# Last down chunk of a two-layer decoder trunk: half of its columns as seven products, in a fixed order

## The chip, the core and the metric

The kernel runs on one core of one Trainium2 chip. The metric is the device time in microseconds of one execution; lower is better. The kernel before was timed three times: 2022.12, 2022.2 and 2024.6 us, median 2022.2 us.

A core has engines with queues of their own: TensorE (PE in the rows, PEld for its weight loads) multiplies, VectorE (DVE) and ScalarE (ACT) work elementwise, GpSimd (POOL) and SyncE (SP) here mostly issue DMAs. Each engine works its queue in the order in which the program was built; engines wait for each other by semaphores.

## What is computed

Two layers over 256 rows of width 2048, in float32. Each layer is a norm, a projection, two mixers, an output projection and a feed-forward part:

```
x = x + mix @ w_out[l]
h = rmsnorm(x, norm2_g[l])
u = jnp.square(jax.nn.relu(h @ w_up[l]))     # 256 x 8192
x = x + u @ w_down[l]                        # 8192 x 2048
```

The change concerns the last line, in both layers.

## The kernel before, in words

**Blocks.** Every weight matrix is cut into blocks of 512 x 512 (four 128-row tiles). A block is loaded by SP (`fetch`, four blocks ahead), then split by `prep` into a rounded half `wh` (two casts on ACT) and the rest `wl` (one subtraction on DVE), because the product is made of three terms: high by high, high by low and low by high. Three sets of `wh` and `wl` exist (`WBUFS`), so the split of block i+3 starts when block i's matmuls have ended.

**Up.** `block_a` computes a block of h @ w_up in 16 matmuls of 512 columns and 16 of 256. Four blocks make 512 columns of u; `up_sum` adds their parts (ACT copies `us`, DVE sums into `ur`), `up_square` applies relu and square on ACT.

**Down.** The 8192 rows of w_down are 8 chunks of 1024; a chunk c needs the u of up parts 2c and 2c+1. A plain block (`block_b`) takes 24 matmuls of 512 columns: 12 for the first 128 rows of u (T = 0), 12 for the second (T = 1). In chunks 0 to 6 the work is cut otherwise: for each half p of the 2048 output columns the chunk is a 2 x 2 by 2 x 2 block product that is made of seven products of 12 matmuls each (`product`, `block_p`) in place of eight. For this DVE and ACT make sums. Of u: `S1`, `S2`, `S3`, `S4` and the splits into high and low halves (`11`, `12`, `22`, `s1` to `s4`, tiles `a...` and `as...`). Of the weights, in a `Super` with four quarter tiles `qx`, `qw`, `qy`, `qz`: the sums x+y and t = (x+y)+z on DVE, and y+z and t+w as accumulating DMAs from POOL's queue. After a product DVE adds its result to x (`add_to`).

**Order.** `BETWEEN` is the order of 22 steps that goes round for each chunk (0 is an up block, other numbers are products, 20 and more belongs to the next chunk). `BESIDE` says after which of these steps each sum, split or load is issued. The chunks 0 to 6 run in a stretch whose order on DVE, ACT, PE and POOL is fixed as written (`manual_schedule`). What stands outside of it is ordered by the scheduler of the language when the kernel is built.

**Last chunk, before.** Chunk 7 has no products: its eight blocks (four column groups n, two row halves kb) are plain `block_b` calls, outside of the fixed stretch, with accumulators in turn from two PSUM pools. Steps of chunk 6 that would start chunk 7's products are left out. After each n DVE adds to x, and in the last layer ACT issues the store of x; in layer 0 the next layer's norm begins (`nxt.chunk(n)`: PE transposes x into bank `hb`, ACT and DVE make the two halves of `hi`, ACT squares x into `jki`).

**Start of the feed-forward part.** The first two up parts run alone, then the product (0, 0, 1), then the weight sums x+y and t of `supers[l, 0, 0]` are issued, then the fixed stretch begins. In that stretch the entry ("t", 0, 22) of `BESIDE` makes t of chunk 0 once more, so this sum stands twice in DVE's queue.

Of the kernel before, what the change touches and what calls it, by code (L numbers as in the profile page):

```python
# [8 lines left out]
F32 = mybir.dt.float32  # L9
F32R = mybir.dt.float32r  # L10
# [7 lines left out]
P = 128  # L18
S = 256
NT = S // P  # L20
# [29 lines left out]

BETWEEN = (0, 0, 2, 0, 5, 6, 0, 7, 3, 0, 11, 4, 0, 15, 0, 16, 13, 12, 17, 0, 21, 14)
NU = len(BETWEEN)
BESIDE = (("up", 0, 6), ("sq", 0, 8), ("load x", 0, 11), ("11", 13), ("S3", 13),
# [8 lines left out]
def trunk(ctx, tc, x, norm1_g, w_in, q_norm_g, k_norm_g, attn_sinks, gla_gate_w,  # L62
          gla_gate_b, gla_norm_g, w_out, norm2_g, w_up, w_down, out):
    nc = tc.nc
# [7 lines left out]
    def bank(name):  # L72
        return misc.tile([P, 512], F32, tag="m", name=name)


    blocks, supers, forms = [], {}, {}
# [59 lines left out]
    for c in range(7):  # L136
        ups = [("up", i, kb) for i in (2 * c + 2, 2 * c + 3) for kb in range(4)]
        if c == 0:
            FFN_ORDER.append(("product", 0, 0, 1))
        for step in BETWEEN:  # L140
            if step == 0:
                FFN_ORDER.append(ups.pop(0))
            elif step < 20 or c < 6:
                FFN_ORDER.append(("product", c + step // 20, step // 10 % 2, step % 10))
    FFN_ORDER += [("down", 7, n, kb) for n in range(4) for kb in range(2)]
    for l in range(DEPTH):
        plan(l)
    NB = len(blocks)
# [58 lines left out]
    now = [0]  # L207

    def add(gen, at):
        side.append([at, gen])  # L210
# [14 lines left out]
    def block_b(accs, lhs, first, last, kts):  # L225

        i = next_block()
        n = blocks[i][2][1] - blocks[i][2][0]
        wh, wl = halves.pop(i)
        for T in range(NT):  # L230
            for k in range(4):
                if kts is None:
                    ah, al = lhs[T][:, k, 0], lhs[T][:, k, 1]
                else:
                    a = lhs[kts[k]]
                    ah = a[:, T * P:(T + 1) * P]
                    al = a[:, S + T * P:S + (T + 1) * P]
                o = accs[T][:, :n]
                nc.tensor.matmul(o, ah, wh[:, k, :n], start=(first and k == 0), stop=False)  # L239
                nc.tensor.matmul(o, ah, wl[:, k, :n], start=False, stop=False)  # L240
                nc.tensor.matmul(o, al, wh[:, k, :n], start=False,  # L241
                                 stop=(last and k == 3))
            if T or n > 264:
                tick()
        prep_to(i + 1 + WBUFS)
# [52 lines left out]
    xs = {}  # L298
# [74 lines left out]
    class Norm:  # L373


        def __init__(self, name, gcols, g0, var):
            self.name, self.gcols, self.g0, self.var = name, gcols, g0, var
            self.ss = sm.tile([P, NT, 4], F32, tag="ss", name=f"ss{name}")
            self.hT = {}
            self.r = None  # L380

        def part(self, n, pr):
            b = bank(f"hb{self.name}{n}{pr}")
# [21 lines left out]
        def chunk(self, n):  # L405
            for pr in range(2):
                self.gain(n, pr, self.part(n, pr))
                yield 1
            self.squares(n)
            if n == 3:  # L410
                yield 1
                self.r = self.rvar() if self.var else self.rstd()

# [453 lines left out]
    def feed_forward(l, norm2):  # L867
# [13 lines left out]
        def up_square(i):  # L881
            nc.scalar.activation(ur[i], ur[i], AF.Relu)
            nc.scalar.activation(ur[i], ur[i], AF.Square)

        def split(name, c, src, tag=None):
            d = fp.tile([P, 4, 2, P], F32R, tag=f"a{tag or name}", name=f"a{name}{l}{c}")
            nc.scalar.activation(d[:, :, 0], src, AF.Copy)
            nc.vector.tensor_tensor(d[:, :, 1], src, d[:, :, 0].bitcast(F32), ALU.subtract)  # L888
            a[name, c] = d

        def beside(c, what, which=0):

            if what == "up":
                up_sum(2 * c + which)
                return
            if what[:4] == "load":
                if c < 7:
                    supers[l, c, which].load(what[5])
                return
            if what == "sq":  # L900
                up_square(2 * c + which)
                return
            if "x" in what or "t" in what or "y" in what:
                if c < 7:
                    supers[l, c, which].sum(what)
                return
            u1, u2 = ur[2 * c], ur.get(2 * c + 1)
            a11, a21 = (u1[:, :, T * P:(T + 1) * P] for T in range(NT))
            if u2 is not None:
                a12, a22 = (u2[:, :, T * P:(T + 1) * P] for T in range(NT))  # L910
            if c == 7:
                if what == "S3":
                    split("21", c, a21, "s1")
                elif what in ("11", "12", "22"):
                    split(what, c, {"11": u1, "12": u2, "22": u2}[what]
                          [:, :, (what == "22") * P:][:, :, :P])
            elif what == "11":
                split(what, c, a11)
            elif what == "S3":
                nc.vector.tensor_tensor(a21, a11, a21, ALU.subtract)  # L920
            elif what == "s3":
                split(what, c, a21)
            elif what == "12":
                split(what, c, a12)
            elif what == "22":
                split(what, c, a22)
            elif what == "S2":
                t = fp.tile([P, 4, P], F32, tag="s2", name=f"s2{l}{c}")
                nc.vector.scalar_tensor_tensor(t, a22, -1.0, a21, ALU.mult, ALU.subtract)
                a["S2", c] = t  # L930
            elif what == "S1":
                nc.vector.tensor_tensor(a11, a["S2", c], a11, ALU.add)
            elif what == "S4":
                nc.vector.tensor_tensor(a12, a["S2", c], a12, ALU.add)
            else:
                split(what, c, {"s1": a11, "s2": a["S2", c], "s4": a12}[what])
# [39 lines left out]
        def go(k0, steps, c0):  # L976

            for k, step in enumerate(steps):
                if step[0] == "up":
                    up(*step[1:])  # L980
                else:
                    product(*step[1:])
                for b in BESIDE:
                    if b[-1] == k0 + k:
                        beside(c0 + 1, *b[:-1])
                    elif b[-1] - NU == k0 + k:
                        beside(c0, *b[:-1])

        ffn = list(FFN_ORDER)
        for i in range(2):  # L990
            for kb in range(4):
                up(*ffn.pop(0)[1:])
                if i == 0 and kb == 1:
                    supers[l, 0, 0].load("xwyz")
            up_sum(i)
            if i == 0:
                nc.vector.tensor_scalar(nr, norm2.r, -1.0, None, ALU.mult)
            up_square(i)
        for b in BESIDE:
            if 8 < b[-1] < NU and b[0] not in ("up", "sq", "x+y", "t") and b[0][:4] != "load":  # L1000
                beside(0, *b[:-1])
        product(*ffn.pop(0)[1:])
        supers[l, 0, 0].sum("x+y")
        supers[l, 0, 0].sum("t")
        with tc.manual_schedule(engines={mybir.EngineType.DVE, mybir.EngineType.Activation,
                                         mybir.EngineType.PE, mybir.EngineType.Pool}):
            for c in range(7):
                n = NU if c < 6 else NU - 1
                go(0, ffn[:n], c)
                del ffn[:n]  # L1010
        beside(7, "22")
        for step in ffn:
            _, c, n, kb = step
            if kb == 0:
                accs = [bank(f"dn{l}{c}{n}{T}") if n % 2 == 0 else
                        acc.tile([P, 512], F32, tag="a", name=f"dn{l}{c}{n}{T}")
                        for T in range(NT)]
            block_b(accs, [a[f"{T + 1}{kb + 1}", c] for T in range(NT)], kb == 0, kb == 1,
                    None)
            if kb == 0:  # L1020
                continue
            for T in range(NT):
                add_to(n, T, accs[T])
                if nxt is None:
                    nc.scalar.dma_start(
                        out[0, T * P:(T + 1) * P, n * 512:(n + 1) * 512], xs[T, n])
            if nxt is not None:
                add(nxt.chunk(n), now[0] + 2)
        return nxt

    norm = Norm("i0", n1cols, 0, False)
# [10 lines left out]

    def start():
        norm.squares(0)
        yield 3
        other_cols()

# [30 lines left out]
```

## Time and profile before

| what | value |
|---|---|
| median of 3 runs | 2022.2 us |
| the profiled execution's own time | 2022.15 us |
| its span, first to last instruction | 2020.4 us |
| PE busy | 2006.2 us, 99% of the span, 10238 matmuls |
| PEld busy | 1694.7 us, 84% |
| DVE busy | 1603.7 us, 79% |
| ACT busy | 1219.2 us, 60% |
| mean granted TensorE clock | 1.000 |
| HBM traffic | 189 GB/s over the span |

The share of busy time is a mean over stages. In the 40 slices of the span DVE's busy tenths are 5 to 7 in the mixers and 8 to 9 in the feed-forward parts. Matmuls overlap: a matmul of 512 columns is shown with 0.39 us, but the next one starts 0.23 us after it, so the step from start to start is what a matmul costs. The same holds, less strongly, on DVE and ACT, whose next instruction starts some 0.09 us before the last one's shown end.

### The profile page before, as it was taken

How to read it: one execution, taken by the hardware profiler on the slowest of the kernel's cores; microseconds unless marked ns; L12 is line 12 of the kernel's file. 1: busy time of each engine (PE TensorE's matmuls, PEld its weight loads, DVE VectorE, ACT ScalarE, POOL GpSimd, SP SyncE). 2: the span in 40 equal slices, each digit the busy share in tenths (PEclk: the TensorE clock that was granted, in tenths of full speed). 3: DMA queues.
4: the chain of work that ended last, by engine and by line, in shares of the span. 5: the costliest groups of instructions: out<-in, count | busy, mean ns of one | idle time of the engine just before them, and what ended most of it. 6: DMA issues, size and time to landing. Idle time of an engine off the chain costs nothing.

```text
span 2020.4 us, 25911 instructions
## 1 busy us (share of the span) xinstructions
PE 2006.2 (99%) x10238; PEld 1694.7 (84%) x10238; DVE 1603.7 (79%) x1452; ACT 1219.2 (60%) x1685; POOL 100.2 (5%) x142
## 2 busy tenths in 40 slices
PE   9999999999999999999999999999999999999999
PEld 7877888888888888888888878888888888888887
DVE  5676565789899998999656765657899999999994
ACT  5575454666666666666555655546666666666663
POOL 3200000000000000000012000000000000000000
PEclk9999999999999999999999999999999999999999
DMA  7554367677878878887555443666877889878874
GB/s 237 173 179 146 108 208 247 202 241 228 288 234 256 262 243 264 240 256 223 188 189 165 160 157 127 201 237 208 255 244 251 248 251 288 244 243 256 236 212 166
DMA packets 205384, 442.59 MB, mean 219 GB/s; under 512 B 7460, under 2 KB 15728, under 8 KB 198096
## 3 DMA queue, kind: packets, MB, share of 16 engines
q1 hardware_dynamic: 194976, 378.82, 53.9%
q0 software_dynamic: 8512, 58.96, 15.7%
q10 hardware_dynamic: 1776, 3.16, 0.4%
q8 instruction: 80, 1.31, 0.3%
q14 instruction: 40, 0.33, 0.0%
HBM read 380.10 MB, written 2.10 MB: 189 GB/s over the span
## 4 chain that ended last, share of the span: by engine, by line
PE 93%; DMA 2%; DVE 2%; ACT 2%; issue 1%; SPq 0%; DVEq 0%; ACTq 0%
PE up L255 22%; PE up L261 11%; PE dn L278 9%; PE dn L276 9%; PE dn L274 9%; PE in L240 6%; PE in L239 6%; PE in L241 6%; PE wo L240 3%; PE wo L241 3%; PE wo L239 3%; PE dn L240 1%; PE dn L241 1%; DMA raw<-in_w_up_dram 1%; PE dn L239 1%; ACT wh L180 1%
## 5 line engine op out<-in xcount | busy, mean ns | idle before, releaser
L185 DVE TENSOR_TENSOR wl<-raw,wh 128x2048 fp32r<-128x2048 f32 (+1 forms) x252 | 560.4, 2224 | 266.6 <-ACT wh L180 262.6
L180 ACT ACTIVATE wh<-raw 128x1024 fp32r<-128x1024 f32 (+2 forms) x516 | 500.8, 1018 | 290.4 <-PE in L241 73.6
L255 PE MATMUL up<-hf,wh 128*128 128x512 f32 x2048 | 504.5, 390 | 0.0
L255 PEld LDWEIGHTS up<-hf,wh 128*128 128x128 f32 x2048 | 376.1, 188 | 71.8
L261 PEld LDWEIGHTS up<-hf,wl 128*128 128x128 f32 x2048 | 275.6, 190 | 18.5 <-DVE wl L185 0.2
L261 PE MATMUL up<-hf,wl 128*128 128x256 f32 x2048 | 281.4, 282 | 0.0
L240 PE MATMUL in<-wl,hi 128*128 128x512 f32 (+1 forms) x640 | 237.2, 372 | 0.4 <-DVE wl L185 0.4
L239 PE MATMUL in<-wh,hi 128*128 128x512 f32 (+1 forms) x640 | 237.6, 374 | 0.0
L241 PE MATMUL in<-wh,hi 128*128 128x512 f32 (+1 forms) x640 | 234.4, 370 | 0.0
L276 PE MATMUL dn<-wl,as 128*128 128x512 f32 x448 | 175.0, 391 | 0.0
L274 PE MATMUL dn<-wh,as 128*128 128x512 f32 x448 | 174.9, 390 | 0.0
L278 PE MATMUL dn<-wh,as 128*128 128x512 f32 x448 | 174.6, 390 | 0.0
L180 ACT ACTIVATE wh<-qx 128x1024 fp32r<-128x1024 f32 x112 | 112.4, 1053 | 49.3 <-DVE qx L97 23.1
L240 PEld LDWEIGHTS in<-wl,hi 128*128 128x128 f32 x640 | 120.1, 188 | 22.4 <-issue 1.5
L239 PEld LDWEIGHTS in<-wh,hi 128*128 128x128 f32 x640 | 120.0, 188 | 21.4 <-issue 1.0
L185 DVE TENSOR_TENSOR wl<-qx,wh 128x2048 fp32r<-128x2048 f32 x56 | 128.1, 2287 | 11.4 <-ACT wh L180 11.4
L241 PEld LDWEIGHTS in<-wh,hi 128*128 128x128 f32 x640 | 119.9, 188 | 20.1 <-issue 0.8
L180 ACT ACTIVATE wh<-qt 128x1024 fp32r<-128x1024 f32 x112 | 112.1, 1050 | 37.4 <-PE up L255 23.3
L278 PE MATMUL dn<-wh,a 128*128 128x512 f32 x336 | 131.2, 391 | 3.4 <-DVE a L888 3.4
L276 PE MATMUL dn<-wl,a 128*128 128x512 f32 x336 | 131.3, 391 | 0.0
L274 PE MATMUL dn<-wh,a 128*128 128x512 f32 x336 | 131.2, 390 | 0.0
L185 DVE TENSOR_TENSOR wl<-qt,wh 128x2048 fp32r<-128x2048 f32 x56 | 128.1, 2287 | 1.3 <-ACT wh L180 1.3
(203 smaller groups left out, 2813.5 us busy)
## 6 DMA issues: line engine op xcount, KB each, us to landing
raw<-in_w_up_dram SPq DMA_DIRECT2D x128, 1024.0 KB, 7.3
raw<-in_w_in_dram SPq DMA_DIRECT2D x62, 1024.0 KB, 5.1
raw<-in_w_out_dram SPq DMA_DIRECT2D x32, 1024.0 KB, 5.0
qx<-in_w_down_dram SPq DMA_DIRECT2D x28, 1024.0 KB, 6.6
qw<-in_w_down_dram SPq DMA_DIRECT2D x28, 1024.0 KB, 5.3
qy<-in_w_down_dram SPq DMA_DIRECT2D x28, 1024.0 KB, 7.6
qz<-in_w_down_dram SPq DMA_DIRECT2D x28, 1024.0 KB, 10.1
qy<-qz POOLq DMA_DIRECT2D x28, 1024.0 KB, 8.2
```

The costliest lines, as they stand in the source:

```text
L180: nc.scalar.activation(wh[:, ks, :n], src[:, ks], AF.Copy)
L185: nc.vector.tensor_tensor(wl[:, :, :n], src, wh[:, :, :n].bitcast(F32), ALU.subtract)
L239: nc.tensor.matmul(o, ah, wh[:, k, :n], start=(first and k == 0), stop=False)
L240: nc.tensor.matmul(o, ah, wl[:, k, :n], start=False, stop=False)
L241: nc.tensor.matmul(o, al, wh[:, k, :n], start=False, stop=(last and k == 3))
L255: nc.tensor.matmul(accs[f], wh[:, k, f * P:(f + 1) * P], rhs[kts[k]], start=(first and k == 0), stop=False)
L261: nc.tensor.matmul(accs[f][:, :S], wl[:, k, f * P:(f + 1) * P], rhs[kts[k]][:, :S], start=False, stop=(last and k == 3))
L274: nc.tensor.matmul(o, ah, wh[:, k], start=(first and k == 0), stop=False, skip_group_check=not first)
L276: nc.tensor.matmul(o, ah, wl[:, k], start=False, stop=False, skip_group_check=not first)
L278: nc.tensor.matmul(o, al, wh[:, k], start=False, stop=(last and k == 3), skip_group_check=not first)
```

## The change

**Chunk 7, columns 1024 to 2047 (p = 1).** They are now made of seven products, as in the chunks before. Product 1 of it stands in chunk 6's round (the step 21 of `BETWEEN`, which was left out before). The columns 0 to 1023 (n = 0 and 1) stay plain blocks. The order of the rest is written out in `LAST`: plain (n 0, kb 0), product 2, plain (0, 1), products 5 and 6, plain (1, 0), products 7 and 3, plain (1, 1), product 4. `BESIDE_LAST` says which sums and splits are issued after each of these ten steps. All of it is inside the fixed stretch. The loads, sums and splits of `BESIDE` now hold for chunk 7 too. All plain accumulators come from one pool. The row split `21` of chunk 7 gets a tile of the `ur` ring.

**Next norm.** It takes the column groups as they are done: 0, 3, then 1 and 2, and counts chunks in place of looking for n = 3.

**Start.** The splits and the difference `11`, `S3`, `s3` of chunk 0 are written right behind the first `up_square`, and the first of the two sums t is gone.

The core of the diff:

```
+LAST = ((0, 0), 2, (0, 1), 5, 6, (1, 0), 7, 3, (1, 1), 4)
+BESIDE_LAST = (("t", "S1", "y+z", "22"), ("s1", "s2"), ("S4",), ("s4",), ("t+w",))
...
-            elif step < 20 or c < 6:
-                FFN_ORDER.append(("product", c + step // 20, step // 10 % 2, step % 10))
-    FFN_ORDER += [("down", 7, n, kb) for n in range(4) for kb in range(2)]
+            else:
+                c1 = c + step // 20
+                FFN_ORDER.append(("product", c1, 1 if c1 == 7 else step // 10 % 2, step % 10))
+    FFN_ORDER += [("product", 7, 1, u) if type(u) == int else ("down", 7, *u) for u in LAST]
...
             up_square(i)
+            if i == 0:
+                for what in ("11", "S3", "s3"):
+                    beside(0, what)
...
         supers[l, 0, 0].sum("x+y")
-        supers[l, 0, 0].sum("t")
...
+            accs = {}
+            for k, step in enumerate(ffn):
+                done = {7: [(3, 1)], 3: [(3, 0)], 4: [(2, 0), (2, 1)]}.get(step[-1], [])
+                if step[0] == "product":
+                    product(*step[1:])
+                else:
...
+                    block_b(accs[n], [a[f"{T + 1}{kb + 1}", c] for T in range(NT)], kb == 0,
+                            kb == 1, None)
...
+                for b in BESIDE_LAST[k:k + 1]:
+                    for what in b:
+                        beside(7, what)
```

DVE's queue in layer 1 at the end of chunk 6 and the begin of chunk 7, before (names: `x` the residual rows, `wl` and `wh` the halves of a block, `a12` and `a22` splits of u):

```order
L941 SCALAR_TENSOR_TENSOR x1_2_109<-dn1611_15574,vf1_10991,x1_2_109 128x512
L185 TENSOR_TENSOR wl446_15861<-raw446_15793,wh446_15860 128x2048
L185 TENSOR_TENSOR wl447_15903<-raw447_15845,wh447_15902 128x2048
L888 TENSOR_TENSOR a1217_15867<-ur115_15832,a1217_15867 128x4x128
L888 TENSOR_TENSOR a2217_15871<-ur115_15832,a2217_15871 128x4x128
L185 TENSOR_TENSOR wl448_15934<-raw448_15876,wh448_15933 128x2048
```

The same place now (`qx`, `qt` the weight sums, `s2` the sum S2):

```order
L190 TENSOR_TENSOR wl449_15893<-qw171_15801,wh449_15892 128x2048
L101 TENSOR_TENSOR qx171_15636<-qx171_15636,qy171_15761 128x2048
L895 TENSOR_TENSOR a1217_15900<-ur115_15863,a1217_15900 128x4x128
L942 SCALAR_TENSOR_TENSOR x1_2_109<-dn1611_15597,vf1_11016,x1_2_109 128x512
L190 TENSOR_TENSOR wl450_15917<-raw450_15877,wh450_15916 128x2048
L930 SCALAR_TENSOR_TENSOR s217_15921<-ur115_15863,ur114_15498 128x512
L190 TENSOR_TENSOR wl451_15950<-qx171_15636,wh451_15949 128x2048
L104 TENSOR_TENSOR qt171_15954<-qx171_15636,qz171_15739 128x2048
L933 TENSOR_TENSOR ur114_15498<-s217_15921,ur114_15498 128x4x128
L895 TENSOR_TENSOR a2217_15958<-ur115_15863,a2217_15958 128x4x128
L942 SCALAR_TENSOR_TENSOR x0_2_107<-dn1712_15961,vf1_11016,x0_2_107 128x512
L190 TENSOR_TENSOR wl452_15978<-qt171_15954,wh452_15977 128x2048
```

The split `a22` stood right behind `a12`; now an add, two block subtractions, S2, the weight sum t and S1 stand between them, and the weight sum x+y stands ahead of both.

ACT's queue in layer 0 where the next norm begins, before (`hi` the next norm's columns, `jki` its squares):

```order
L402 ACTIVATE jki100_8045,ssi1_2877<-x0_0_89 128x512
L180 ACTIVATE wh223_8003<-raw223_7931 128x1024 x2
L402 ACTIVATE jki101_8047,ssi1_2877<-x1_0_91 128x512
L402 ACTIVATE jki110_8137,ssi1_2877<-x0_1_98 128x512
L180 ACTIVATE wh224_8049<-raw224_7966 128x1024 x2
L369 ACTIVATE hi10_7997<-hbi100_7992,n1cols_118 128x256
L402 ACTIVATE jki111_8139,ssi1_2877<-x1_1_100 128x512
L369 ACTIVATE hi11_8000<-hbi100_7992,n1cols_118 128x256
L369 ACTIVATE hi12_8027<-hbi101_8022,n1cols_118 128x256
L180 ACTIVATE wh225_8095<-raw225_8008 128x1024 x2
```

And now:

```order
L374 ACTIVATE hi10_8061<-hbi100_8056,n1cols_118 128x256
L374 ACTIVATE hi11_8064<-hbi100_8056,n1cols_118 128x256
L185 ACTIVATE wh226_8067<-qz071_7738 128x1024 x2
L374 ACTIVATE hi12_8092<-hbi101_8087,n1cols_118 128x256
L374 ACTIVATE hi13_8095<-hbi101_8087,n1cols_118 128x256
L407 ACTIVATE jki100_8110,ssi1_2877<-x0_0_89 128x512
L407 ACTIVATE jki101_8112,ssi1_2877<-x1_0_91 128x512
L185 ACTIVATE wh227_8114<-raw227_8041 128x1024 x2
```

In both orders up to four small steps stand between two casts `wh`. Before, all blocks here were plain, with 24 matmuls each; now `wh225`, `wh226` and `wh227` belong to products 7 and 3, with 12 matmuls each, and to the plain block (1, 1).

## Rows read from the trace of the kernel before

**Rows 1.** The cores: span, and mean granted TensorE clock.

```profile
core 0: 2020.4 us, clock 1.000
```

**Rows 2.** The page's first part: busy us (share of the span) xinstructions.

```profile
PE 2006.2 (99%) x10238; PEld 1694.7 (84%) x10238; DVE 1603.7 (79%) x1452; ACT 1219.2 (60%) x1685; POOL 100.2 (5%) x142
```

**Rows 3.** PE's waits: engine line, waited for: us in total, times, longest.

```profile
PE dn L278 <- DVE a L888: 3.4, 2, 1.9
...
PE dn L240 <- DVE wl L185: 1.3, 2, 0.7
```

**Rows 4.** Timeline of PE, layer 1's end: start, us, line, out<-in [idle <-releaser].

```profile
1958.13 0.39 PE L274 MATMUL dn<-wh,a 128*128 128x512 f32 x1
...
1960.85 0.39 PE L274 MATMUL dn<-wh,as 128*128 128x512 f32 x1
...
1969.16 0.63 PE L239 MATMUL dn<-wh,a 128*128 128x512 f32 x2
...
1977.37 0.61 PE L239 MATMUL dn<-wh,a 128*128 128x512 f32 x2
1978.64 0.50 PE L240 MATMUL dn<-wl,a 128*128 128x512 f32 x1 [0.66 <-DVE wl L185]
1978.97 0.40 PE L241 MATMUL dn<-wh,a 128*128 128x512 f32 x1
```

**Rows 5.** Timeline of DVE, the same stretch.

```profile
1962.72 0.74 DVE L941 SCALAR_TENSOR_TENSOR x<-dn,vf,x 128x512 f32<-128x512 f32 x1
1963.38 2.28 DVE L185 TENSOR_TENSOR wl<-qt,wh 128x2048 fp32r<-128x2048 f32 x1
...
1970.93 2.29 DVE L185 TENSOR_TENSOR wl<-raw,wh 128x2048 fp32r<-128x2048 f32 x1 [2.40 <-ACT wh L180]
1973.14 1.69 DVE L878 TENSOR_TENSOR ur<-up,us 128x256 f32<-128x256 f32 x4
1974.74 0.74 DVE L941 SCALAR_TENSOR_TENSOR x<-dn,vf,x 128x512 f32<-128x512 f32 x1
1976.29 2.29 DVE L185 TENSOR_TENSOR wl<-raw,wh 128x2048 fp32r<-128x2048 f32 x1 [0.81 <-ACT wh L180]
```

**Rows 6.** Timeline of DVE, layer 0, begin of the feed-forward part's fixed stretch.

```profile
387.27 2.28 DVE L100 TENSOR_TENSOR qt<-qx,qz 128x2048 f32<-128x2048 f32 x1
...
395.53 0.68 DVE L929 SCALAR_TENSOR_TENSOR s<-ur,ur 128x512 f32<-128x512 f32 x1
398.41 2.29 DVE L185 TENSOR_TENSOR wl<-raw,wh 128x2048 fp32r<-128x2048 f32 x1 [2.20 <-ACT wh L180]
400.62 2.29 DVE L100 TENSOR_TENSOR qt<-qx,qz 128x2048 f32<-128x2048 f32 x1
402.82 0.69 DVE L932 TENSOR_TENSOR ur<-s,ur 128x512 f32<-128x512 f32 x1
403.42 0.69 DVE L888 TENSOR_TENSOR a<-ur,a 128x512 fp32r<-128x512 f32 x1
```

**Rows 7.** Timeline of ACT, the same stretch.

```profile
396.37 2.01 ACT L180 ACTIVATE wh<-raw 128x1024 fp32r<-128x1024 f32 x2 [1.43 <-DMA raw<-in_w_up_dram]
```

**Rows 8.** Timeline of PE, the same stretch.

```profile
401.84 0.40 PE L276 MATMUL dn<-wl,a 128*128 128x512 f32 x1
...
404.17 0.50 PE L278 MATMUL dn<-wh,a 128*128 128x512 f32 x1 [1.93 <-DVE a L888]
```

**Rows 9.** Timeline of ACT, layer 0's end, next norm's steps.

```profile
986.30 0.63 ACT L402 ACTIVATE jki<-x 128x512 f32<-128x512 f32 x1 [3.02 <-DVE x L941]
...
997.17 0.84 ACT L369 ACTIVATE hi<-hbi,n1cols 128x256 fp32r<-128x256 f32 x2 [1.78 <-DVE hi L370]
```

**Rows 10.** Timeline of DVE, the same stretch.

```profile
997.68 0.88 DVE L370 SCALAR_TENSOR_TENSOR hi<-hbi,n1cols,hi 128x256 fp32r<-128x256 f32 x2 [0.54 <-ACT hi L369]
```

**Rows 11.** Waits between 960 and 1030 us: total, times, longest.

```profile
ACT hi L369 <- DVE hi L370: 6.6, 3, 2.4
```

**Rows 12.** Timeline of PE, the same stretch: six of the next norm's transposes.

```profile
992.90 0.81 PE L387 MATMUL hbi<-ident,x 128*128 128x128 f32 x6
```

**Rows 13.** The page's DMA issues: engine, count, KB each, median us to landing.

```profile
qy<-qz POOLq DMA_DIRECT2D x28, 1024.0 KB, 8.2
```

More of the change, by code (lines that the diff above doesn't have):

```diff
@@ L379, in __init__ @@
             self.hT = {}
-            self.r = None
+            self.r, self.chunks = None, 0
         def part(self, n, pr):
@@ L409, in chunk @@
             self.squares(n)
-            if n == 3:
+            self.chunks += 1
+            if self.chunks == 4:
                 yield 1
@@ L885, in split @@
         def split(name, c, src, tag=None):
-            d = fp.tile([P, 4, 2, P], F32R, tag=f"a{tag or name}", name=f"a{name}{l}{c}")
+            d = fp.tile([P, 4, 2, P], F32R, tag=tag or f"a{name}", name=f"a{name}{l}{c}",
+                        bufs=3 if tag else 1)
             nc.scalar.activation(d[:, :, 0], src, AF.Copy)
@@ L896, in beside @@
             if what[:4] == "load":
-                if c < 7:
-                    supers[l, c, which].load(what[5])
+                supers[l, c, 1 if c == 7 else which].load(what[5])
                 return
@@ L903, in beside @@
             if "x" in what or "t" in what or "y" in what:
-                if c < 7:
-                    supers[l, c, which].sum(what)
+                supers[l, c, 1 if c == 7 else which].sum(what)
                 return
@@ L910, in beside @@
                 a12, a22 = (u2[:, :, T * P:(T + 1) * P] for T in range(NT))
[L911 to L917, printed above, removed]
+            if c == 7 and what == "S3":
+                split("21", c, a21, "ur")
+            if what == "11":
                 split(what, c, a11)
@@ L998, in feed_forward @@
             up_square(i)
+            if i == 0:
+                for what in ("11", "S3", "s3"):
+                    beside(0, what)
         for b in BESIDE:
-            if 8 < b[-1] < NU and b[0] not in ("up", "sq", "x+y", "t") and b[0][:4] != "load":
+            if 8 < b[-1] < NU and b[0] in ("12", "S2"):
                 beside(0, *b[:-1])
@@ L1007, in feed_forward @@
             for c in range(7):
[L1008 to L1028, printed above, removed]
+                go(0, ffn[:NU], c)
+                del ffn[:NU]
+            accs = {}
[4 more added lines that the diff above has]
+                else:
+                    _, c, n, kb = step
+                    if kb == 0:
+                        accs[n] = [acc.tile([P, 512], F32, tag="a", name=f"dn{l}{c}{n}{T}")
+                                   for T in range(NT)]
+                    block_b(accs[n], [a[f"{T + 1}{kb + 1}", c] for T in range(NT)], kb == 0,
+                            kb == 1, None)
+                    done = [(n, T) for T in range(NT)] if kb else []
+                    for n, T in done:
+                        add_to(n, T, accs[n][T])
+                for b in BESIDE_LAST[k:k + 1]:
+                    for what in b:
+                        beside(7, what)
+                for n, T in done:
+                    if nxt is None:
+                        nc.scalar.dma_start(
+                            out[0, T * P:(T + 1) * P, n * 512:(n + 1) * 512], xs[T, n])
+                if nxt is not None and done and step[-1] != 7:
+                    add(nxt.chunk(done[0][0]), now[0] + 2)
         return nxt
@@ L1044, in start @@
         norm.squares(0)
+        norm.chunks += 1
         yield 3
```

## Prediction, made before the changed kernel was timed

> **What bounds the kernel now.** I read the cores' line first, for the clock and the span [rows 1], then the shares [rows 2]: TensorE is busy for 99% of the span, VectorE for 79%. The profiled execution took 2022.15 us around a span of 2020.4 us, and 2022.15 is within 0.1 us of the median of the three runs, so sums made against it hold for the median. Next I read PE's waits [rows 3]. In the two feed-forward parts there are two kinds: twice 1.9 us until a split of u is ready, at the begin of the fixed stretch, and twice 0.7 us until a `wl` is ready, in chunk 7. Everything else is matmul after matmul, so a matmul removed is worth its step, as long as nobody is late. Then I read the stretch that is changed, in layer 1, engine by engine. On PE a product of 12 matmuls takes 2.72 us from start to start (1958.13 to 1960.85), 0.227 each; a plain block of 24 takes 5.44 [rows 4]. On DVE a subtraction `wl` or a weight sum takes 2.20 us of its queue (400.62 to 402.82), an add to x 0.66 (1962.72 to 1963.38), a sum or split of u 0.60 (402.82 to 403.42) [rows 5, 6]. So a product costs PE 2.72 us, and DVE one `wl` and one add, 2.86 us, before any sum is made. DVE has slack only because plain blocks and up blocks stand between the products.
>
> **What is removed.** Per layer 192 matmuls become 84 + 96 = 180: 12 x 0.227 = 2.72 us saved, 5.44 us for both. The old wait of PE in chunk 7 goes too: from 1977.37 two matmuls are due within 0.45, and the third starts at 1978.64, so 0.82 us, with 0.10 more because the step after a wait is 0.33 in place of 0.23 [rows 4]: 0.92 per layer.
>
> **What is added to DVE's queue, layer 1.** I follow DVE's and PE's queues forward from 1969.16, where the last up block ends and nothing has changed yet. PE now does product (7,1,1) to 1971.88, product 4 of chunk 6 to 1974.60, plain (0,0) to 1980.04. On DVE the rows from 1970.93 to 1976.29 stay, as the same steps stand there in the same order, a `wl` last [rows 5]. Then, back to back: x+y at 1978.49, `a12` at 1980.69, ready with 0.69 and 0.06 until PE sees it (as 403.42 to 404.17 [rows 6, 8]) at 1981.44. Product 2 wants it for its third matmul at 1980.50: PE waits **0.94**, and the product ends at 1983.81. DVE goes on: add 1981.29, `wl` of plain (0,1) 1981.95, S2 1984.15, `wl` of product 5 1984.75, weight sum t 1986.95, S1 1989.15, `a22` 1989.75, visible at 1990.50. Plain (0,1) wants its `wl` at 1984.04 and gets it at 1984.30 (**0.26**); it wants `a22` for its second half at 1987.35 and gets it at 1990.50 (**3.15**). It ends at 1992.87. Product 5 wants the low half of `as1` at 1993.33. DVE's `wl` ahead of it cannot start before ACT has cast the sum t, 1989.28 to 1991.29 (a cast takes 2.01 [rows 7]), so `as1` comes at 1994.28 (**0.95**). Behind that I find no wait: product 6 and the plain blocks give DVE time. The waits come to 5.30, with four late steps of 0.10 to 5.7 us. Layer 1: 5.7 - 0.92 - 2.72 = **+2.1 us**.
>
> **Layer 0** has the same, +2.1, and then the next norm in the same queues. Two more places:
> - Plain (1,1). After `as1` DVE makes `as2` and, behind its cast, a `wl` at 1995.0. From the adds at 1997.2 (on layer 1's clock) I count: two adds, S4, an add, a `wl`, a split, an add, 6.04 us; a half of `hi`, 0.52; ACT's next half, 0.36; a cast, 2.03; a `wl`, 2.20; `hi` on DVE, 0.52, and on ACT, 0.36; two squares, 1.26 [rows 9]; a cast, 2.03; a `wl`, 2.33. This is 2014.9. ACT and DVE take turns on a bank of `hi`, as they do now: ACT waited three times for DVE's half, 6.6 us in all, once 1.78, and DVE for ACT's 0.54 [rows 9 to 11]. PE wants that `wl` at 2011.4: product 5 ends at 1996.65, then come product 6, plain (1,0), products 7 and 3 (2.72 + 5.44 + 2.72 + 2.72 = 13.60), eight transposes, 0.9 [rows 12], and one matmul. PE waits **3.5 us**.
> - The next layer's first block. Columns n = 1 and 2 are now the last to be done, and the block needs n = 1 second. From the restart at 2014.85 PE has 5.3 + 2.72 + 5.44 us of matmuls, 2.6 of transposes, and wants the second n = 1 tile 1.8 later, at 2032.7. DVE must do five `wl`, five adds, five halves of `hi` and 0.7 of small steps first: 17.0 us, to 2031.8, which alone would cost nothing. With the turns of ACT and DVE (each of three casts stands behind a `hi` or a square, and the `wl` behind it) I come to 2036.9: **4.2 us**. The ends of this term are 0 and 4.2; I take 4.2, since such turns cost waits in rows of before.
>
> Layer 0: 2.1 + 3.5 + 4.2 = **+9.8 us**.
>
> **Edits that cost nothing.** The removed sum t (387.27) frees 2.2 us of DVE, but DVE then stands idle 2.20 us at 398.41 for a cast which waits for a DMA of an up block [rows 6, 7]. The sum that stays, at 400.62, is the one right ahead of the late split, so PE's wait there, 2.1 us (401.84 + 0.23 to 404.17 [rows 8]), stays. Its ends are 0 and 4.2 us gained for both layers; I take 0. The earlier `11`, `S3`, `s3` change no order in any queue. The two more accumulating DMAs per layer land some 8.2 us after their issue [rows 13]; in the queue their readers come 15 us later and more. SP loads as many blocks as before, four quarters in place of four blocks. The store at the very end is one add and one DMA behind the last matmul, as before.
>
> **Sum.** 2022.15 + 2.1 + 9.8 = **2034 us**. Its own range is 2030 to 2038: the 4.2 of the norm partly saved, or each of seven waits longer by half a microsecond.
>
> **Rivals.**
> A. *TensorE stays the bound.* Then the saved matmuls and the old waits are all: 2022.15 - 5.44 - 1.84 = 2014.9, or 2010.7 if the waits at the start go as well. For it speaks the share of 99% against 79% [rows 2]; against it that the 79% is a mean, and that the order puts seven DVE steps between `a12` and `a22`. It decides at plain (0,1): DVE would have to be 3.15 us earlier there, more than one `wl`. The Trainium skill (Perfetto Trace Analysis, Identifying the Most-Contended Engine) says to take the engine of highest occupancy first; by that rule the time would fall, as here. No row speaks for its use over a stretch where the product's 2.72 us meet 2.86 us of DVE.
> B. *The next norm hides as it does now.* Only the waits in front of it stay, in both layers: 2022.15 + 4.2 = 2026.4. For it: before, PE lost nothing to the norm's steps. Against it: they stood beside blocks of 5.44 us, now beside products.
> C. *The clock falls.* The granted clock was 1.000 throughout [rows 1], the higher level of 2.4 GHz, and stayed there over PE's waits of 1.9 us. Three new waits are over 3 us. If the lower level held for one plain block after each, 24 x 0.227 = 5.4 us each, it would be 2039 with one and 2050 with three. The Trainium skill (TensorE: Matmul & The Clock Gate, Why this matters for your kernels) warns of idle gaps between bursts of matmuls that take the clock to half; no row here shows a fall.
>
> **How the numbers follow.** Forecast 0.72, A 0.08, B 0.10, C 0.07, and 0.03 that gains and waits cancel. Within 0.2% (4 us) is about what a measurement of this kernel can tell from no change. Faster: A, 0.08. Same: 0.03 and a third of B, 0.06. Slower: the rest, 0.86. The range, 2028 to 2041, holds the forecast, a part of B and the milder part of C, and leaves A and the worst of C out.
>
> **What would show it.** In the new profile PE's matmuls are 24 fewer. PE's waits should name DVE: `a` or `as` splits four times with the longest over 3 us in each layer, and a `wl` and `hi` in layer 0 alone. DVE should have no idle time from the sum x+y to `a22` (12 us). Layer 0's part should account for some 10 us of the loss and layer 1's for 2. I am wrong if PE has no wait over 1 us in chunk 7, if the time is under 2026, or if the clock is below 1.000 in the windows behind the waits.

## The result and the profile after

| | before | after |
|---|---|---|
| median | 2022.7 us | 2041.5 us (2038.4 to 2043.0) |
| ratio | | 1.009, 95% interval 1.0078 to 1.0102 |
| profiled execution, its own time | 2022.15 us | 2038.39 us |
| mean granted TensorE clock, profiled execution | 1.000 | 0.998 |

(The median of before is that of the executions beside the changed kernel.) The change costs 18.8 us. The forecast was 2034 with a range of 2028 to 2041: the sign is right, the profiled execution lies inside, the median half a microsecond above the top. (The kernel before, too, took half a microsecond more beside this measurement than the 2022.15 us that the forecast was added to: 2022.15 + 18.8 = 2041.0, the top itself.)

The page of the changed kernel, its cores' line and its shares; they answer to [rows 1, 2]:

```profile
core 0: 2036.3 us, clock 0.998
...
PE 2005.0 (98%) x10214; PEld 1689.8 (83%) x10214; DVE 1635.3 (80%) x1482; ACT 1234.6 (61%) x1705; POOL 106.2 (5%) x146
```

TensorE has the 24 matmuls less, and the kernel is longer all the same. The shares have hardly moved, so the loss isn't to be read there. It is in PE's waits, which answer to [rows 3] (columns: who waits, for whom, us in total, times, longest):

```profile
PE dn L283 <- DVE a L895: 6.2, 4, 2.6
PE dn L246 <- DVE a L895: 5.9, 2, 3.0
...
PE dn L245 <- DVE wl L190: 2.8, 1, 2.8
PE in L246 <- DVE hi L375: 2.3, 2, 1.2
PE in L244 <- ACT hi L374: 1.0, 1, 1.0
PE dn L283 <- DVE as L895: 0.8, 1, 0.8
PE dn L279 <- DVE x L944: 0.4, 1, 0.4
PE dn L244 <- ACT wh L185: 0.3, 1, 0.3
```

The old `wl` wait [rows 3] is gone, and the new ones are those that the prediction had listed, plus two small ones, for x and for a cast `wh`. The wait for the split `as1`, however, is there once only, in layer 0. DVE's queue in layer 1 answers to [rows 5]: from x+y to `a22`, nine instructions without a gap (no brackets), 1990.01 to 2001.96.

```profile
1990.01 2.29 DVE L101 TENSOR_TENSOR qx<-qx,qy 128x2048 f32<-128x2048 f32 x1
1992.21 0.69 DVE L895 TENSOR_TENSOR a<-ur,a 128x512 fp32r<-128x512 f32 x1
...
1998.48 2.28 DVE L104 TENSOR_TENSOR qt<-qx,qz 128x2048 f32<-128x2048 f32 x1
2000.68 0.68 DVE L933 TENSOR_TENSOR ur<-s,ur 128x512 f32<-128x512 f32 x1
2001.28 0.68 DVE L895 TENSOR_TENSOR a<-ur,a 128x512 fp32r<-128x512 f32 x1
```

And PE's queue there, which answers to [rows 4] (start, duration, instruction; in brackets the wait and who ended it). These are plain block (0,1)'s second half and, for comparison, the same place in layer 0:

```profile
988.56 0.50 PE L246 MATMUL dn<-wh,a 128*128 128x512 f32 x1 [2.96 <-DVE a L895]
988.89 0.39 PE L244 MATMUL dn<-wh,a 128*128 128x512 f32 x1
989.12 0.40 PE L245 MATMUL dn<-wl,a 128*128 128x512 f32 x1
...
2002.02 0.79 PE L246 MATMUL dn<-wh,a 128*128 128x512 f32 x1 [2.96 <-DVE a L895]
2002.61 0.63 PE L244 MATMUL dn<-wh,a 128*128 128x512 f32 x1
2003.04 0.63 PE L245 MATMUL dn<-wl,a 128*128 128x512 f32 x1
```

The wait is the same to 0.01 us. Behind it, however, the step from matmul to matmul is 0.23 us in layer 0 and 0.43 in layer 1: the clock has gone to its lower level, 1.2 GHz, for 12 matmuls, and the first step behind the wait is 0.59 in place of 0.33. The same in windows of 10 us (columns: window, length, busy time and instructions of five engines, granted clock, DMA share, GB/s):

```profile
990.00:1000.00 10.00, 9.19 (x42) 7.27 (x42) 9.68 (x9) 5.57 (x7) 0.86 (x1) 1.00 0.67 132
...
1990.00:2000.00 10.00, 8.25 (x34) 5.85 (x32) 10.00 (x8) 4.90 (x6) 0.88 (x1) 1.00 0.58 103
2000.00:2010.00 10.00, 7.98 (x23) 6.34 (x24) 7.34 (x8) 5.05 (x6) 0.87 (x1) 0.66 0.62 171
```

A granted clock below 1.000 behind a wait is one of the three signs by which the prediction wanted to be called wrong, and here it is: 0.66. So two questions were left. Do the waits carry the loss, or the clock? And is VectorE's queue really what is waited for?

### The profile page after: what moved, and what is told of

The parts are those of the page before. It is cut to its first block, busy times and chain, and to the rows that moved or that the text cites. A ratio compares the mean times of both kernels' runs of the same rounds, so it can differ in the third digit from the quotient of the medians.

```text
span 2036.3 us, 25923 instructions
## 1 busy us (share of the span) xinstructions
PE 2005.0 (98%) x10214; PEld 1689.8 (83%) x10214; DVE 1635.3 (80%) x1482; ACT 1234.6 (61%) x1705; POOL 106.2 (5%) x146
## 4 chain that ended last, share of the span: by engine, by line
PE 88%; DMA 5%; DVE 3%; ACT 2%; issue 2%; SPq 0%; ACTq 0%; DVEq 0%
PE up L260 19%; PE up L266 10%; PE dn L283 9%; PE dn L279 9%; PE dn L281 9%; PE in L244 6%; PE in L245 6%; PE in L246 6%; DMA raw<-in_w_up_dram 3%; PE wo L245 3%; PE wo L246 3%; PE wo L244 3%; DVE wl L190 2%; ACT wh L185 2%; PE sc L542 1%
## 5 line engine op out<-in xcount | busy, mean ns | idle before, releaser
L190 DVE TENSOR_TENSOR wl<-raw,wh 128x2048 fp32r<-128x2048 f32 (+1 forms) x244 | 541.7, 2220 | 254.7 <-ACT wh L185 248.5
L185 ACT ACTIVATE wh<-raw 128x1024 fp32r<-128x1024 f32 (+2 forms) x500 | 484.6, 1017 | 272.6 <-PE in L246 76.0
L283 PE MATMUL dn<-wh,as 128*128 128x512 f32 x480 | 187.4, 390 | 0.8 <-DVE as L895 0.8
L279 PE MATMUL dn<-wh,as 128*128 128x512 f32 x480 | 187.8, 391 | 0.4 <-DVE x L944 0.4
L281 PE MATMUL dn<-wl,as 128*128 128x512 f32 x480 | 187.8, 391 | 0.0
L185 ACT ACTIVATE wh<-qt 128x1024 fp32r<-128x1024 f32 x120 | 120.2, 1050 | 50.6 <-PE up L260 23.3
L185 ACT ACTIVATE wh<-qx 128x1024 fp32r<-128x1024 f32 x120 | 120.5, 1053 | 49.5 <-DVE qx L101 23.1
L283 PE MATMUL dn<-wh,a 128*128 128x512 f32 x360 | 140.8, 391 | 6.2 <-DVE a L895 6.2
L190 DVE TENSOR_TENSOR wl<-qx,wh 128x2048 fp32r<-128x2048 f32 x60 | 137.1, 2284 | 11.4 <-ACT wh L185 11.4
L281 PE MATMUL dn<-wl,a 128*128 128x512 f32 x360 | 140.7, 391 | 0.0
L279 PE MATMUL dn<-wh,a 128*128 128x512 f32 x360 | 140.7, 391 | 0.0
L190 DVE TENSOR_TENSOR wl<-qt,wh 128x2048 fp32r<-128x2048 f32 x60 | 136.9, 2282 | 2.0 <-ACT wh L185 2.0
## 6 DMA issues: line engine op xcount, KB each, us to landing
qz<-in_w_down_dram SPq DMA_DIRECT2D x30, 1024.0 KB, 10.1
```

Source lines behind the costliest of these rows:

```text
L185: nc.scalar.activation(wh[:, ks, :n], src[:, ks], AF.Copy)
L190: nc.vector.tensor_tensor(wl[:, :, :n], src, wh[:, :, :n].bitcast(F32), ALU.subtract)
L279: nc.tensor.matmul(o, ah, wh[:, k], start=(first and k == 0), stop=False, skip_group_check=not first)
L281: nc.tensor.matmul(o, ah, wl[:, k], start=False, stop=False, skip_group_check=not first)
L283: nc.tensor.matmul(o, al, wh[:, k], start=False, stop=(last and k == 3), skip_group_check=not first)
```

## Experiments: where the loss lies

**One layer at a time.** The order, the loads and the sums of chunk 7 are made to depend on the layer; the start edits stay in both.

```
+SEVEN = (0,)          # (1,) in the second kernel
...
+        if l not in SEVEN:
+            return order + [("down", 7, n, kb) for n in range(4) for kb in range(2)]
+        return order + [("product", 7, 1, u) if type(u) == int else ("down", 7, *u) for u in LAST]
```

Layer 0:

> The new last chunk in layer 0 alone; layer 1's last chunk is as before; the edits at the start stay in both layers. Theory (VectorE's queue sets the time, each layer with its own price): in the changed kernel's trace TensorE is 10.8 us behind the kernel before at the end of layer 0 and does not win or lose anything in layer 1 but 0.7 us at its start, so +11.5 us, 2033.7 us, granted clock 1.000. Rival (the loss is mostly a clock that falls behind waits of over 3 us, of which layer 0 has two or three): the clock shows below 1.000 in layer 0 and the time is 2037 us or more.

Measured: 2038.35 us, ratio 1.0075 (1.0061 to 1.0089). Layer 1:

> The new last chunk in layer 1 alone; layer 0's is as before; the edits at the start stay in both layers. Theory: waits of TensorE of 0.9, 0.2, 3.1 and 1.0 us less the saved 2.72 us and the old waits of 0.92 us give +2.1 us, with 1.4 us for the two starts +3.5 us, 2025.6 us at a clock of 1.000; where the clock falls behind the wait of 3.1 us, as in the changed kernel's profiled execution, 2 to 5 us more, 2028 to 2031 us. Rival (the clock fell in the changed kernel because of what went before in layer 0): no fall, 2025.6 us in every execution.

Measured: 2027.2 us (2025.3 to 2030.3), ratio 1.0019 (1.0010 to 1.0028). The losses against before, 14.7 and 3.6 us, add up to 18.3, within the noise the 18.8 of both: no sign that the layers disturb each other. For layer 1 the theory holds with the fall of the clock: the profiled execution has one behind `a22`, and another behind the start's wait in layer 0, and takes 2029.2 us, the median lies between the figures without a fall and with one, and the rival's 2025.6 in every execution is out. In layer 0 the time is 4.7 us above the waits' 2033.7, where the rival put it. The windows of layer 0 alone show why:

```profile
400.00:410.00 10.00, 7.80 (x34) 6.23 (x33) 8.41 (x8) 4.61 (x6) 0.00 (x0) 0.83 0.57 174
985.00:995.00 10.00, 7.03 (x21) 5.30 (x20) 8.66 (x8) 3.76 (x5) 0.86 (x1) 0.69 0.62 154
...
1010.00:1020.00 10.00, 6.95 (x22) 5.07 (x23) 6.83 (x7) 7.64 (x12) 0.00 (x0) 0.83 0.25 81
```

The clock fell behind the start's wait (8 matmuls at 0.43 us), behind that for `a22` (13) and behind that in plain block (1,1) (6): 27 steps that are 0.20 us too long, 5.4 us. In the changed kernel's profile none of these three waits was followed by a fall, though the two in chunk 7 have the same lengths (3.36 and 3.28 us from start to start here, 3.35 and 3.27 there) and the start's is even longer there (3.01 against 2.60). So the waits in chunk 7 come out alike; whether the clock falls behind them changes from execution to execution.

**VectorE's sums taken away.** In chunk 7, x+y and t are not made, nor t+w; products 2, 4 and 6 read unsummed quarters. (t+w is a transfer; its issue stands far behind `a22`, so leaving it out can't shorten the wait for `a22`.)

```
+            if c == 7 and ("x" in what or "t" in what):
+                return
```

> The changed kernel with VectorE's two weight sums of chunk 7, x+y and t, and the accumulating DMA t+w left out; products 2, 4 and 6 multiply unsummed quarters, so the output is another. TensorE does the same matmuls. Theory (VectorE's queue is the bound in chunk 7): the queue is 4.4 us shorter in each layer before a22, so TensorE's wait of 3.1 us for it falls below 1.1 us in both layers, no wait over 1.2 us is left in layer 1, the clock stays 1.000 there, and layer 1's chunk 7 costs less than before; layer 0 keeps the waits for the next norm (some 3 and 4 us). By the queues followed forward the time falls by 6.4 us without the clock's part, to 2032 us, and to 2030 us or less with it. Rival (the transfers, the accumulating ones above all, are late, or the turns with ScalarE are the bound): the wait for a22 stays over 2 us and the time over 2036 us.

Measured: 2031.6 us, ratio 1.0044 (1.0031 to 1.0058). PE's waits:

```profile
PE dn L247 <- DVE wl L192: 2.8, 1, 2.8
...
PE in L248 <- DVE hi L377: 2.4, 2, 1.2
PE dn L248 <- DVE a L897: 1.4, 2, 0.7
```

The two waits of 3.0 us for `a22` are 0.7 now, no matmul of layer 1 runs at the lower clock, and layer 0's `wl` and `hi` waits stay. From the last matmul of the last up block to the last matmul of all, layer 1 takes 47.15 us before, 51.58 after, 46.26 here. VectorE's queue is what was waited for. The last figure also says what seven products win in layer 1 in this order with 4.4 us of VectorE's work for nothing: 0.9 us, of 2.72 saved. Other orders were not tried beyond the next run.

**A wait moved.** In layer 1 alone, `a22` is made ahead of t, S1 and y+z.

```
-BESIDE_LAST = (("t", "S1", "y+z", "22"), ("s1", "s2"), ("S4",), ("s4",), ("t+w",))
+BESIDE_LAST = (("22", "t", "S1", "y+z"), ("s1", "s2"), ("S4",), ("s4",), ("t+w",))
```

> As the run of layer 1 alone, but the split a22 is issued ahead of the sum t, S1 and y+z. Theory (all of VectorE's work up to product 5 is the debt, so a wait that is removed in one place comes back at the next): the wait of 3.1 us for a22 falls to 0.5, and product 5 waits 2.5 and 1.9 us for its two splits s1 in place of 1.0; the time stays within 1 us of the run of layer 1 alone, 2027 us. Rival (one split stands at a bad place): about 3 us less, 2024 us.

Measured: 2029.2 us, ratio 1.0029 (1.0018 to 1.0041). The wait did move, to product 5:

```profile
1991.82 0.50 PE L284 MATMUL dn<-wh,as 128*128 128x512 f32 x1 [2.25 <-ACT as L899]
1992.16 0.40 PE L286 MATMUL dn<-wl,as 128*128 128x512 f32 x1
1994.23 0.79 PE L288 MATMUL dn<-wh,as 128*128 128x512 f32 x1 [1.67 <-DVE as L900]
1994.82 0.63 PE L284 MATMUL dn<-wh,as 128*128 128x512 f32 x1
```

The rival's 2024 is out: the debt of VectorE's queue came back at the next split. The time itself is 2.0 us above layer 1 alone, where at most 1 us had been expected. (The intervals of the two overlap; that the two new waits side by side are worse for the clock is only a guess.)

**The next norm, begun later**, in layer 0 alone:

```
-                        add(nxt.chunk(done[0][0]), now[0] + 2)
+                        if step[:1] == ("down",) and step[2] == 0:
+                            held = done[0][0]
+                        else:
+                            add(nxt.chunk(done[0][0]), now[0] + 2)
+                            if step[-1] == 3 and step[0] == "product":
+                                add(nxt.chunk(held), now[0] + 2)
```

> As the run of layer 0 alone, but the next norm's columns n = 0 are begun behind product 3 and not behind the plain block (0,1). Theory (the next norm is a debt that VectorE and ScalarE carry into the next layer): the wait of 3.0 us in plain block (1,1) and the 0.6 us ahead of it go, the next layer's first block waits longer by about 1 us, and at the transposes of x another 0.9 us comes; some 1.8 us less than the run of layer 0 alone, and up to 1.5 us more where the clock had fallen behind the wait that goes: 2035 to 2036.5 us. Rival (the wait in plain block (1,1) is a loss by itself): 3.6 us less and the clock's 1.2 us, 2033.5 us. Rival 2 (the whole debt returns): no change, 2038.3 us.

Measured: 2036.3 us, ratio 1.0063 (1.0047 to 1.0078). The trace is in part as the theory has it: no wait in plain block (1,1), and instead new ones at the transposes. The next layer's first block waits no longer than in layer 0 alone, 3.3 us of idle time in both, where 1 us more had been expected:

```profile
PE in L249 <- ACT hi L379: 2.1, 2, 1.4
PE hbi L397 <- DVE x L957: 1.4, 2, 1.1
PE in L251 <- DVE hi L380: 1.2, 1, 1.2
```

From layer 0's last up block to the 97th matmul of the next layer's blocks it takes 84.6 us, and 86.7 in layer 0 alone, with about as many matmuls at the lower clock (17 and 19 of 512 columns). So some 2 us of the 3.5 are won and the rest comes back. In time alone the two kernels' intervals overlap.

## Experiments: the start, and the clock

**Start edits alone**, chunk 7 as before in both layers (`SEVEN = ()`):

> Only the edits at the start of the feed-forward part: the first of the two sums t is gone, and 11, S3, s3 are written earlier; chunk 7 is as before in both layers. Theory (the prediction put these edits at nothing): 2022.2 us, within 1 us. Rival (read from the changed kernel's trace, where TensorE's wait at the start grew by 0.7 us in each layer): +1.4 us, 2023.6 us. Third possibility (VectorE's time there is on the path): up to 4.2 us faster, 2018 us.

Measured: 2024.2 us, ratio 1.0002 (0.9993 to 1.0011): no change that can be measured. The interval goes from 1.4 us less to 2.2 us more, so the gain of 4.2 us is out and the rival's 1.4 us is not. **The other sum dropped:**

```
         supers[l, 0, 0].sum("x+y")
+        supers[l, 0, 0].sum("t")
...
-                    elif b[-1] - NU == k0 + k:
+                    elif b[-1] - NU == k0 + k and (c0, b[:2]) != (0, ("t", 0)):
```

> Chunk 7 as before in both layers; of the two sums t at the start the first, right behind x+y, is kept, and the second, right ahead of the late split a12, is dropped. Theory (VectorE's queue between the cast and a12 is what TensorE waits for at the start, and the changed kernel dropped the sum that stood in idle time): a12 comes 2.2 us earlier in each layer, the wait of TensorE of 1.9 to 2.8 us falls under 1 us, and with it goes the fall of the clock behind it; 3 to 5 us faster than the kernel before, 2019 us. Rival (what TensorE waits for there is the transfer of the up block behind the cast, whichever sum is dropped): within 1 us of the kernel before.

Measured: **2018.5 us, ratio 0.9978 (0.9969 to 0.9986)**: faster than before and after. DVE's queue there, to be held against [rows 6]:

```profile
398.40 2.29 DVE L195 TENSOR_TENSOR wl<-raw,wh 128x2048 fp32r<-128x2048 f32 x1 [2.17 <-ACT wh L190]
400.61 0.69 DVE L948 TENSOR_TENSOR ur<-s,ur 128x512 f32<-128x512 f32 x1
401.21 0.69 DVE L900 TENSOR_TENSOR a<-ur,a 128x512 fp32r<-128x512 f32 x1
```

The idle 2.17 us, in which VectorE waits for the cast, is the same; behind it `a12` comes 2.2 us earlier, and PE's waits for `a` at the start, 1.9 and 1.5 us (3.4 in total in [rows 3]), are gone in both layers. The rival is out. Inside the changed kernel the same exchange is worth as much, within the noise. The changed kernel was run again beside it:

> The changed kernel once more, beside the next two on one chip. Theory (waits worth 12 us, 1.4 us at the starts, and falls of the clock behind the waits of over 2 us that differ from execution to execution): 2038 to 2043 us, median 2041 us, slower executions with a lower mean clock. Rival (the loss is the waits alone): all executions within 1 us of one another, 2036 us.

Measured: 2042.1 us; its four executions took 2037.6, 2041.8, 2042.5 and 2044.1 us at mean clocks of 0.998, 0.996, 0.996 and 0.994. The spread is the theory's, not the rival's.

> The changed kernel, but of the two sums t at the start the first is kept and the second, right ahead of the late split a12, is dropped. Theory (the start's part adds up with the rest): as in the run with chunk 7 as before, 4 to 6 us less than the changed kernel, 2036 us, and TensorE's waits for a at the start gone in both layers; the waits in chunk 7 unchanged (0.9, 0.2, 3.1, 1.0 us and the norm's). Rival (time won at the start is taken back by chunk 7's queue): within 1.5 us of the changed kernel.

Measured: 2035.75 us, ratio 1.0060 (1.0046 to 1.0074), against 1.0088 (1.0074 to 1.0102) for the changed kernel: 6.4 us less. The start's part adds up with the rest. This trace shows one thing more. In layer 1 the clock stays at 1.000 here, and PE waits there for `as1` and, further on, for an add to x:

```profile
2004.76 0.50 PE L283 MATMUL dn<-wh,as 128*128 128x512 f32 x1 [0.81 <-DVE as L895]
...
2016.07 0.47 PE L279 MATMUL dn<-wh,as 128*128 128x512 f32 x1 [0.59 <-DVE x L944]
```

From the last up block to the end layer 1 takes 50.08 us here, against 51.58 in the changed kernel's profile: in the end that fall of the clock cost 1.5 us.

**One wait, by itself.** On the kernel of 2018.5 us, two additions whose result nobody reads stand in VectorE's queue ahead of layer 1's first plain block of chunk 7:

```
+                if (l, c0, k) == (1, 6, 19):
+                    q = supers[1, 6, 1].t
+                    for n in (4, 1):
+                        nc.vector.tensor_tensor(q["x"][:, :n], q["x"][:, :n], q["z"][:, :n],
+                                                ALU.add)
```

> The kernel with chunk 7 as before and the other sum dropped (2018.5 us, no wait over 2 us but one at 251), with two idle additions on VectorE, 2.75 us in all, ahead of the first plain block of layer 1's chunk 7 (their result is read by nobody). Theory (a wait costs itself and, in part of the executions, a fall of the clock): TensorE's wait of 0.7 us there becomes 2.3, +1.6 us, 2020.1 us where the clock holds, and 1.2 to 2.6 us more where it falls, so executions between 2019.5 and 2023 us, median 2021 us. Rival (a wait costs only itself): 2020.1 us, spread as without it.

Measured: 2022.2 us (2020.0 to 2024.5; 2021 and at most 2023 had been expected), ratio 0.9993 (0.9984 to 1.0002). In the trace the wait is 2.69 us in place of 0.66:

```profile
1977.29 0.77 PE L250 MATMUL dn<-wl,a 128*128 128x512 f32 x1 [2.69 <-DVE wl L195]
1977.86 0.63 PE L251 MATMUL dn<-wh,a 128*128 128x512 f32 x1
...
1980.42 0.56 PE L251 MATMUL dn<-wh,a 128*128 128x512 f32 x1
1980.82 0.40 PE L249 MATMUL dn<-wh,a 128*128 128x512 f32 x1
```

2.0 us more of wait (1.6 had been expected) cost 3.0 us (difference of the ratios, times 2022) to 3.7 us (difference of the medians). By the times alone the excess over 2.0 isn't shown, since each of the two ratios is uncertain by some 1.7 us. The clock says more: the trace has 7 matmuls at the lower level behind the wait, and the two executions at a mean clock of 1.000 took 2020.0 and 2020.9 us, 2.2 us above the median of those at 1.000 without the additions, while the median of the other nine is 1.9 us higher still. So where the clock holds, the wait costs its length. Without the two additions 9 of 11 executions had a mean clock of 1.000, with them 2 of 11; part of that can be the chip, for the two kernels ran on different ones, and beside the first the kernel before had 1.000 in 11 of 17 executions, beside the second in 4 of 15.

## Why the prediction was right, and where it was off

| term | predicted | measured |
|---|---|---|
| matmuls saved | 24, 5.4 us | 24 |
| PE waits for `a12`, `wl`, `a22`, `as1` (layer 0) | 0.94, 0.26, 3.15, 0.95 | 0.90, 0.23, 3.12, 0.97 |
| wait in plain (1,1), layer 0 | 3.5 | 3.5 (0.42 + 3.04) |
| next layer's first block | 4.2 (0 to 4.2) | 3.7 (1.06 + 1.33 + 1.35) |
| layer 0 in all, clock at 1.000 | +9.8 | +10.1 (72.9 to 83.0) |
| layer 1 in all | +2.1 | +2.9 (47.15 to 50.08, changed kernel with the other sum, clock at 1.000); +4.4 (to 51.58) with one fall of the clock |
| start edits | 0 (0 to 4.2 gain) | not to be told from 0 alone |
| clock | 1.000 | 0.994 to 0.998 |

(Waits as in the changed kernel's trace, layer 0: the step from start to start, less 0.23. Layer 0 goes from its last up block to the 97th matmul of the next layer's blocks.)

**The mechanism is shown.** VectorE's queue is the bound in chunk 7: in the window 1990 to 2000 it is busy 10.00 of 10.00 us, and with its sums taken away the waits go. In layer 0 the four waits of the first two products and plain block (0,1) came where the two queues followed forward had put them, to within 0.05 us, the wait in plain (1,1) too, and those of the next layer's first block to within 0.5 us. In layer 1 the first three came; the fourth, for `as1`, came only where the clock held. That rivals A and B fall follows from the same rows: PE lost to VectorE, and to the norm. Rival A's rule, the engine of highest occupancy first, would have given 2014.9. The Trainium skill (Perfetto Trace Analysis, Optimization Strategy) itself adds that a kernel may have several regimes with another engine most contended in each; this trace agrees, with 80% for VectorE over the span and 100% in that window.

**One wait was missed.** In layer 1 the prediction followed the queues as far as product 5 and found no wait behind that. The trace with the clock at 1.000 has one for an add to x at 2016.07, 0.75 us. That is most of the 0.8 us by which the waits of layer 1 exceed the forecast (2.9 against 2.1).

**The term that was mis-sized is the clock.** The prediction held it apart as rival C, with 0.07, because the clock had stayed at 1.000 over waits of 1.9 us in the one trace of before. That trace was one execution. In the runs beside the experiments the kernel before itself took 2021.3 to 2026.4 us at mean clocks from 1.000 down to 0.997, so falls were in its times already. The changed kernel has more and longer waits, so more falls: in the profiled execution one, 12 matmuls that are 0.20 us too long, 2.4 us. VectorE catches up meanwhile: the wait for `as1`, 0.97 us, is gone behind it, and the one for x is 0.56 us in place of 0.75, so that 1.5 us are left of the fall. With the 0.8 us above these are the 2.3 us by which layer 1 was off. The other executions lose more: from 0.998 to 0.996 the mean clock loses 0.002 x 2036 = 4.1 us, and the medians of its two series lie 3 to 5 us above their profiled executions. So the prediction's third sign of being wrong, a clock below 1.000 behind a wait, did show, and on this term it was wrong. C was right as to its kind and wrong as to its form. It is not an alternative to the forecast, but a part of it in most executions, and a fall behind one wait costs 1.2 to 2.6 us (6 to 13 matmuls, 0.20 each), not 5.4, and less where VectorE catches up. The Trainium skill (TensorE: Matmul & The Clock Gate, Why this matters for your kernels) warns of idle gaps between bursts of matmuls; the runs agree in part, with a fall behind 17 of the 33 longest gaps counted below and none behind the other 16.

**The start edits** were put at nothing for the right reason (the sum that stays is the one ahead of the split), and the other choice won the 4.2 us that the prediction had named as the bound. That bound was a little too high for the waits alone: it took them as twice 2.1 us, from a longest wait of 1.9, but the two are 1.9 and 1.5 (3.4 in total in [rows 3]), 3.8 us from start to start; that the rest of the 4.2 is fewer falls of the clock is likely, not shown. In the changed kernel's profile PE's wait at layer 0's start was longer than in [rows 8], 2.6 us against 1.9; the same kernel run again has 2.0 there, so this differs from execution to execution, and whether the start edits add to it stays open. With the same in layer 1 it makes 1.4 of the profiled 16.2 us.

**Why the range missed the median.** Its top was the forecast's waits and one expensive fall. The profiled execution is 4.4 us above the forecast: 0.8 for the waits of layer 1, 1.5 for its fall, 0.3 for layer 0 and 1.4 for the starts make 4.0. The median is another 3.2 us higher, at a lower mean clock (0.996 to 0.997). That the median came out at the top of the range, and not well above it, is in part luck: the 5.4 us that rival C took for one fall is about what several smaller ones cost.

## What to carry over

- Where an edit trades work of the busiest engine for work of a second one, take both queues over that stretch, instruction by instruction, and follow them forward; the shares over the whole span say nothing of it. In layer 0 this gave four waits to 0.05 us and those of the next norm to half a microsecond. Follow them to the end of the stretch: the wait that was missed lies where the working stopped.
- A wait of TensorE of over 2 us can cost more than its length: here the clock fell behind 17 of the 33 longest. Price the falls in as a part of the forecast, and read the clock from the spread of the executions, not from one trace.
- Of two instructions that do the same, drop the one ahead of what is waited for, not the one that stands in idle time.

## What the runs showed of the hardware

In the twelve traces, from 200 us on, 33 steps between neighbouring matmuls were 2.18 us or longer; behind 17 of them the step went from 0.23 to 0.43 us, at once or up to six matmuls later, for 6 to 13 matmuls, and back. Of the 18 that were over 3 us, 11 were followed by such a fall; of the 15 from 2.18 to 3.0, six. A single step of 1.6 us or less was followed by none, but several close together were: in the kernel with the later norm, 1.02 and 1.56 us at 1036.92 and 1039.28 were followed by eight matmuls at the lower clock, and with `a22` early, 2.64 and 2.07 us (the first is one of the six) by 13. The same wait at the same place, 3.35 us for `a22`, was followed by 0 to 13 matmuls at the lower level in different executions. What decides it stays open.
